# A choice of experts without GpSimd arithmetic, a gather ahead of the first weight splits, and buffers cleared on ScalarE

## The chip, the cores and the metric

The kernel runs on one core of a Trainium2 chip. The metric is device time in microseconds, from the first to the last instruction and what lies around them; shorter is better. The engines are called as the profile calls them: PE (TensorE, matmuls), DVE (VectorE), ACT (ScalarE), POOL (GpSimd) and SP (SyncE). Each has a queue of instructions of its own and works through it in order. DMAs are issued from the queues of SP, ACT and POOL. What an engine needs from another it waits for on semaphores.

## The reference

One step of an encoder layer over 576 tokens: 512 frames of one stream and 64 of another. The first half mixes tokens (sparse attention and a convolution branch). The second half is a mixture of experts, and the change lies where the one passes into the other:

```python
x = layer_norm(ALPHA * x + (1 + g1) * mix, ln1_g, ln1_b)
h2 = x * (1 + sc2) + sh2
# hier_moe(h2): the best of 4 groups, in it the best 2 of 4 experts
gl = hf @ w_group + b_group;  g_idx = argmax(gl);  g_w = max(softmax(gl))
rl = hf @ w_router + b_router
top_val, top_idx = lax.top_k(in_group, 2)
w_top = softmax(top_val) * g_w
# per expert: silu(h @ gate) * (h @ up) * weight, then @ down, summed over the two
x = layer_norm(ALPHA * x + (1 + g2) * moe, ln2_g, ln2_b)
```

There are 16 experts; each has a gate-and-up matrix of 1024 x 512 and a down matrix of 256 x 1024. All is float32.

## The kernel before

Tokens lie in five tiles of 128 (the last has 64), `t` = 0 to 4. Products that need full precision split each float32 operand into a rounded high part and a low part: `split_into` copies the high part on ACT (L139) and subtracts it on DVE (L140), and `mm3` (L144 to L146) makes three matmuls of them.

*Around the choice.* For each tile, `ln1` normalises the rows `xn[t]` and multiplies them with the routers on PE (L849); L850 adds the bias on DVE. `h2_rows` (L856) scales the rows on DVE and sums them with a DMA of POOL into the scratch tensor `h2_scr` (L857), from which the experts gather. `ax_rows` multiplies `xn[t]` by ALPHA's row in place (L900) and sums it with a DMA of POOL into `z_scr` (L901), the start of the final residual. Tiles 0 and 1 multiply on DVE, tiles 2 to 4 on POOL. `route` then picks groups, experts and places with many small DVE operations (L919 to L978), once for tiles 0 to 2 and once for tiles 3 and 4. Its result for the four fixed experts is `idt` (L1011, called `routed` in the code). The exponential for the weights is on ACT (L1030), and L1031 on DVE waits for it. Further DVE operations (L1054 to L1074) put the other twelve experts in order of their size; `order` (L1072) is read by SP, which then loads the weights of the experts it names.

*Experts.* `gather` (L1125) fetches up to 128 rows of `h2_scr` into one of three buffers `xg`; POOL makes its descriptors. The buffers are cleared first (L1080, on POOL). Two of them lie in the buffers of `h2`, so they wait for the DMAs of `h2_rows`. `table` then writes the slot of every token with ten small scatters from POOL (L1263). `rows_in` transposes the gathered rows on PE (L1140), copies the high part on ACT (L1145) and subtracts on DVE (L1146), all into `xhl`. An expert's gate-and-up product goes in four quarters (`step`, six matmuls each); `hidden` (L1163, L1164), `turned` (L1170), `down` (L1188) and a scatter-add into `z_scr` (L1203) follow. On PE the next expert's first two quarters come ahead of the turn and the down product of the one before.

*Weights.* Six 512 KB pieces per expert stream through a ring of 24 places (six buffers of four). A gate-and-up piece is split ahead by `split_ahead`: three sets of split buffers are free at the start (`room[False]`), and a fourth, which lies in the buffers of `xn[4]` and `ohr`, counts as `room[True]`. The fourth split therefore waits for the DMA that sums `xn[4]` into `z_scr`. When a piece has been split, SP loads a later expert's piece into its place.

*Slots.* One pool of seven large buffers holds the ring's six and `xhl`. The last ring buffer takes the place of `rows1`, which L856 reads last. `xhl` takes that of `xn03`, which holds `xn[0]` to `xn[3]`; in the compiled program its first write, L1145, waits for the four DMAs of L901 that sum these tiles.

*Order.* A planner orders each engine's queue by program order and by when its own cost model has an instruction ready. `issue_after(ins)` queues a block's instructions behind `ins` on that engine and is no wait. `manual_schedule` keeps the expert part of PE, DVE and ACT in the order written. In the compiled program POOL's queue runs: sums of `h2` and `z` with the three multiplications and the clears among them, the three first gathers, the ten scatters of the table.

Of the kernel before, what the change touches and what calls it, by code (L numbers as in the profile page):

```python
# [10 lines left out]
F32 = mybir.dt.float32  # L11
# [3 lines left out]
AF = mybir.ActivationFunctionType  # L15
OP = mybir.AluOpType
# [8 lines left out]
NT = 5  # L25
# [33 lines left out]
def encoder_step(ctx: ExitStack, tc: tile.TileContext, a, o):  # L59
    nc = tc.nc  # L60
    V, S, G, PE, SY = nc.vector, nc.scalar, nc.gpsimd, nc.tensor, nc.sync
# [67 lines left out]
        raw_load[0] = (eng or SY).dma_start(raw, src).ins  # L129
        return raw  # L130

    raw_load, split_copy = [None], [None]

    def split(raw, shape, tag="w", bufs=3):
        return split_into([wp.tile(shape, F32R, name=tag + p, tag=tag + p, bufs=bufs) for p in ("hi", "lo")], raw)
# [1 line left out]
    def split_into(parts, raw):  # L137
        hi, lo = parts
        split_copy[0] = S.copy(hi, raw).ins  # L139
        V.tensor_tensor(lo, raw, hi, op=OP.subtract)  # L140
        return hi, lo

    def mm3(out, lh, ll, rh, rl, start, stop):
# [750 lines left out]
    ax_sums = []  # L894


    def ax_rows(t, behind):
        n = TS[t]
        with tc.issue_after(behind):
            (G if t > 1 else V).tensor_tensor(xn[t][0:n], xn[t][0:n], axr[0:n], op=OP.mult)  # L900
            ax_sums.append(G.dma_start(dap(z_d, t * 128 * D, [[D, n], [1, D]]), xn[t][0:n], accum_op=OP.add).ins)  # L901

    mb = late.tile([128, NT + 1, 16], BF, name="mb", bufs=1)
# [76 lines left out]
    for t in range(NT):  # L980
        n = TS[t]
        sl = slice(128 * t, 128 * t + n)
        po = acc("o1")
        if t == 4:
            with tc.issue_after(trs[1]):
                for k0 in range(0, KT, 2):
                    sample_product(po, k0, 2, ms, *wo[k0 // 2])
        else:
            for k in range(KT):
                wh, wl = wo[k // 2]  # L990
                mm3(po, mh[:, k, sl], ml[:, k, sl], wh[:, k % 2, :], wl[:, k % 2, :], k == 0, k == KT - 1)
        residual(t, po, 1)
        ln1(t)
        if 0 < t < 4:
            h2_rows(t - 1)
            if t < 3:
                ax_rows(t - 1, normed[-1][0])
    ohr = late.tile([128, 2, NT, 128], F32R, name="ohr", tag="ohr", bufs=1)
    route(0, 3)
    h2_rows(3)  # L1000
# [15 lines left out]
    routed = token_columns(pid[:, 0:NFIX], 0, NFIX)  # L1016
    pids = late.tile([128, 2, NVAR], F32, name="pids", tag="bw", bufs=1)
    V.tensor_copy(pids[:, 0, :], pid[:, NFIX:NE])

    for t in range(2, NT):  # L1020
        ax_rows(t, routed)


    w12 = late.tile([128, NT, 2], F32, name="w12", bufs=1)
# [52 lines left out]

    xg = [late.tile([128, D], F32, name="xg", tag=tag, bufs=2) for tag in ("h2", "h2", "xg")]
    for x in xg:
        G.memset(x, 0.0)  # L1080


    ring = []
# [174 lines left out]
    def table():  # L1258
        V.tensor_copy(pay.bitcast(F32)[:, :, :, 1], w12)
        for t, j in [(t, j) for t in range(NT) for j in range(2)]:  # L1260
            n = TS[t]
            with tc.issue_after(gathers[2]), tc.issue_after(ax_sums[-1]):
                st = G.indirect_dma_start(out=ids_d, out_offset=bass.IndirectOffsetOnAxis(ap=slt[0:n, t, j:j + 1], axis=0),  # L1263
                                          in_=pay[0:n, t, j, :], in_offset=None)
            for other in scat:
                tc.declare_no_dep(st.ins, other.ins, reason="every slot is given to one row")
            scat.append(st)
# [68 lines left out]
                load_down(number(n), k, n.down[k])  # L1336

    steps = [(x, c) for x in units for c in range(4) if len(x.experts) == 1]
    room = {False: 3, True: 1}
    owed = [0]  # L1340


    def split_ahead():
        while steps and len(steps[0][0].experts[0].gate_up) > steps[0][1]:
            x, c = steps[0]
            fourth = room[False] <= owed[0]
            if not room[fourth]:
                return
            steps.pop(0)
            room[fourth] -= 1  # L1350
            x.parts.append([next_split(x.experts[0].gate_up[c], fourth)])
            x.sets.append(fourth)
            follow_gate_up(x.experts[0], c)

    def gather_next():
        n = len(gathers)
        for x in units:
            for b, ar in x.blocks:
                if b == n:
                    return gather(b, ar[0])  # L1360
# [12 lines left out]
        x.parts, x.sets = [], []  # L1373
    LA = 2
    load_first(2)
    for _ in range(3):
        gather_next()
    table()
    with tc.manual_schedule(engines={mybir.EngineType.PE, mybir.EngineType.DVE, mybir.EngineType.Activation}):
        first_loads(3)  # L1380
        with tc.issue_after(routed):
            split_ahead()
        rows_in(0)
        pend, over = [], overflow()

        def product(p):
            p.y = gate_row(p.ar[2], p.ar[3])
            p.pd = down(p.hT, p.dns)
            for y in p.experts:
                y.left -= 1  # L1390
                if y.left == 0:
                    follow_down(y)
            add_rows(p.y, p.pd, p.ar[0])

        for u, x in enumerate(units):
            if u == 2:
                for y in units:
                    i = y.es[0] - NFIX
                    if 0 <= i < NPAIR:
                        c = G.value_load(order[0:1, NVAR + i:NVAR + i + 1], min_val=3 * (NE + NFIX), max_val=3 * (2 * NE - 1))  # L1400
                        y.blocks[1] = (y.blocks[1][0], place_ids(c, G))
                    if len(y.es) == 2:
                        y.blocks[0] = (y.blocks[0][0], static_args(y.es))
                token_columns(cols[:, 0, NFULL:NVAR], NFIX + NFULL, NE)
            owed[0] = int(u + 1 < len(units) and len(units[u + 1].es) == 2)
            blocks = []
            for b, _ in x.blocks:
                p = Unit()
                p.b, p.experts = b, x.experts
                p.ar = dict(x.blocks)[b]  # L1410
                p.dns = [y.down for y in x.experts]
                blocks.append(p)
            for y in x.experts:
                y.left = len(blocks)
            nxt = units[u + 1].blocks[0][0] if u + 1 < len(units) else None

            def step(c, p, last=True):
                if c == 0:
                    p.pg = acc("pg")
                if len(x.experts) == 1:  # L1420
                    gate_up(p.pg, p.b, c, x.parts[c])
                else:
                    gate_up(p.pg, p.b, c, [y.gate_up[c] for y in x.experts])
                    for y in x.experts:
                        follow_gate_up(y, c)
                if c == 3:
                    p.hm = hidden(p.pg, p.ar[1])
                if u > NFIX and not (u + c) % 2:
                    next(over, None)
                if last:  # L1430
                    freed(c)

            def freed(c):
                if len(x.experts) == 1:
                    room[x.sets[c]] += 1
                elif c == 3:
                    room[False] += 1
                split_ahead()

            def rows(b):  # L1440
                if b is not None:
                    whole = any(len(y.es) == 2 and y.blocks[0][0] == b for y in units)
                    if whole:
                        assert room[False]
                        room[False] -= 1
                        owed[0] = 0
                    rows_in(b, whole)
                    if len(gathers) <= b + LA:
                        gather_next()

            def turn_next(i):
                if i < len(pend):
                    pend[i].hT = turned(pend[i].hm)

            def product_next(i):
                if i < len(pend):
                    product(pend[i])

            if len(blocks) == 1:
                p = blocks[0]  # L1460
                step(0, p)
                step(1, p, False)
                turn_next(0)
                freed(1)
                rows(nxt)
                product_next(0)
                turn_next(1)
                step(2, p)
                product_next(1)
                step(3, p)  # L1470
            else:
                p, q = blocks
                step(0, p, False)
                rows(q.b)
                step(1, p, False)
                turn_next(0)
                turn_next(1)
                product_next(0)
                step(0, q)
                step(1, q)  # L1480
                product_next(1)
                step(2, p, False)
                step(3, p, False)
                rows(nxt)
                step(2, q)
                step(3, q)
            pend = blocks
        rows3 = slot([128, 2, D], name="rows3")
        brow(rows3[:, 0], a["ln2_g"], 0, SY)
        brow(rows3[:, 1], a["ln2_b"], 0, SY)  # L1490
        for i in range(len(pend)):
            turn_next(i)
            product_next(i)
# [83 lines left out]
```

## Time and profile before

| | us |
|---|---|
| median of 3 runs (860.08 to 865.51) | 863.53 |
| the profiled execution's own time | 862.35 |
| its span, first to last instruction | 860.7 |
| PE busy | 774.9 (90%) |
| DVE busy | 639.8 (74%) |
| ACT busy | 358.3 (42%) |
| POOL busy | 137.9 (16%) |

The profile is one execution. A row of a timeline gives the start, the length in us, the engine, the line, the operation with its output and inputs, how many were merged, and in brackets how long the engine stood idle before it and what ended that. A row of the chain of waits gives the start, the length, and what the program's end waited for at that time. Groups of instructions give the count, the busy time and the mean in ns of one. Waits are put down to what came last by the profile's own inference.

### The profile page before, as it was taken

The page shows a single profiled execution, that of the slowest core. Times are in us where ns is not written, and L with a number is a line of the kernel's source. Part 1 is how long each engine was busy: PE and PEld are TensorE (multiplying, and loading weights), DVE is VectorE, ACT ScalarE, POOL GpSimd, SP SyncE. Part 2 cuts the span into 40 slices and gives each one's busy share as a digit, 9 for nine tenths or more (in the row PEclk, how much of TensorE's full clock was granted, in tenths as well). Part 3 has the DMA queues.
Part 4 walks back from the last instruction along what each step waited for, and adds up shares of the span by engine and source line. Part 5 has one row for each costly group of instructions (what it writes and reads, how often), then busy time and mean ns, then how long its engine had stood idle before and what let it go on. Part 6 is the DMA issues. An engine that isn't in the chain of part 4 may idle for free.

```text
span 860.7 us, 13259 instructions
## 1 busy us (share of the span) xinstructions
PE 774.9 (90%) x4827; PEld 633.9 (74%) x4827; DVE 639.8 (74%) x1255; ACT 358.3 (42%) x654; POOL 137.9 (16%) x172
## 2 busy tenths in 40 slices
PE   4899999999999999999999999999835999999910
PEld 3788888887878989988999799978734676645400
DVE  1569999989998999999995426539793886555416
ACT  3243232333335435568633943312423664434205
POOL 2300000300200000000100001110556223212220
PEclk9999999999999999999999999999857899999965
DMA  9997754482432333343433108585996998799425
GB/s 290 340 365 236 223 175 150 114 226 82 144 107 74 101 91 103 91 127 92 130 103 103 40 1 299 200 268 162 222 307 164 342 360 275 206 353 378 130 49 200
DMA packets 108865, 159.70 MB, mean 186 GB/s; under 512 B 9714, under 2 KB 67210, under 8 KB 108800
## 3 DMA queue, kind: packets, MB, share of 16 engines
q1 hardware_dynamic: 94464, 120.38, 42.9%
q0 software_dynamic: 12736, 34.26, 15.4%
q10 hardware_dynamic: 1600, 4.22, 1.3%
q8 instruction: 38, 0.62, 0.3%
q14 instruction: 27, 0.22, 0.1%
HBM read 143.65 MB, written 26.13 MB: 197 GB/s over the span
## 4 chain that ended last, share of the span: by engine, by line
PE 56%; DVE 10%; DMA 4%; ACT 3%; issue 2%; another core or an unknown queue 1%; POOL 0%; POOLq 0%; SPq 0%; DVEq 0%; ACTq 0%
PE acc L242 6%; PE acc L244 6%; PE acc L243 6%; PE pd L1188 5%; PE pg L144 3%; PE pg L146 3%; PE pg L1158 3%; PE pg L145 2%; PE tm L144 2%; PE po L673 2%; PE tm L146 2%; PE tm L145 2%; DMA z_scr<-yo,idt 2%; PE pxt L1140 2%; PE o L144 2%
## 5 line engine op out<-in xcount | busy, mean ns | idle before, releaser
L600 DVE SCALAR_TENSOR_TENSOR y<-ue,dwT,y 128x604 f32<-128x604 f32 (+17 forms) x232 | 183.4, 827 | 1.9 <-ACT y L598 1.5
L242 PE MATMUL acc<-hh,wlo 128*128 128x288 f32 (+1 forms) x504 | 152.7, 303 | 1.4 <-DVE wlo L140 1.4
L243 PE MATMUL acc<-hh,whi 128*128 128x288 f32 (+1 forms) x504 | 149.9, 298 | 0.0
L244 PE MATMUL acc<-hl,whi 128*128 128x288 f32 (+1 forms) x504 | 148.5, 298 | 0.0
L139 ACT CAST whi<-wraw 128x1024 fp32r<-128x1024 f32 (+1 forms) x72 | 75.1, 1045 | 159.6 <-PE acc L244 72.9
L140 DVE TENSOR_TENSOR wlo<-wraw,whi 128x1024 fp32r<-128x1024 f32 (+1 forms) x72 | 87.4, 1214 | 38.1 <-ACT whi L139 38.0
L242 PEld LDWEIGHTS acc<-hh,wlo 128*128 128x128 f32 (+1 forms) x504 | 94.3, 187 | 16.7 <-issue 8.7
L243 PEld LDWEIGHTS acc<-hh,whi 128*128 128x128 f32 (+1 forms) x504 | 94.3, 187 | 2.8 <-issue 2.6
L244 PEld LDWEIGHTS acc<-hl,whi 128*128 128x128 f32 (+1 forms) x504 | 93.6, 187 | 2.3 <-issue 2.1
L140 DVE TENSOR_TENSOR wlo<-ring,whi 128x1024 fp32r<-128x1024 f32 x30 | 36.4, 1223 | 21.3 <-ACT whi L139 20.8
L144 PE MATMUL tm<-wlo,hh 128*128 128x512 f32 x128 | 50.5, 397 | 0.4 <-DVE wlo L140 0.4
L145 PE MATMUL tm<-whi,hh 128*128 128x512 f32 x128 | 50.4, 394 | 0.0
L146 PE MATMUL tm<-whi,hl 128*128 128x512 f32 x128 | 49.8, 392 | 0.0
L139 ACT CAST whi<-ring 128x1024 fp32r<-128x1024 f32 x30 | 31.3, 1049 | 34.3 <-PE pg L146 23.3
L1188 PE MATMUL pd<-ring,hT 128*128 128x512 f32 x96 | 44.4, 606 | 1.0 <-ACT hT L1172 0.5
L242 PE MATMUL acc<-oh,wlo 128*128 128x288 f32 x128 | 38.6, 302 | 1.5 <-DVE gt L757 1.1
L242 PE MATMUL acc<-yh,wlo 128*128 128x288 f32 x128 | 38.4, 301 | 0.1
L243 PE MATMUL acc<-yh,whi 128*128 128x288 f32 x128 | 38.4, 301 | 0.0
L244 PE MATMUL acc<-yl,whi 128*128 128x288 f32 x128 | 38.2, 302 | 0.1
L1203 POOL DMA_INDIRECT z_scr<-yo,idt x16 | 26.5, 1656 | 73.2 <-DMA z_scr<-yo,idt 29.7
L243 PE MATMUL acc<-oh,whi 128*128 128x288 f32 x128 | 38.0, 298 | 0.0
L244 PE MATMUL acc<-ol,whi 128*128 128x288 f32 x128 | 37.8, 298 | 0.0
(474 smaller groups left out, 1743.7 us busy)
## 6 DMA issues: line engine op xcount, KB each, us to landing
ring<-in_w_gate_up_dram SPq DMA_DIRECT2D x62, 512.0 KB
wraw<-in_w_in_dram SPq DMA_DIRECT2D x48, 512.0 KB
wada<-in_w_ada_dram SPq DMA_DIRECT2D x32, 512.0 KB
ring<-in_w_down_dram SPq DMA_DIRECT2D x32, 512.0 KB
wada<-in_w_ada_dram SPq DMA_DIRECT2D x32, 256.0 KB
gates_scr<-glg POOLq DMA_DIRECT2D x16, 288.0 KB
gt<-gates_scr POOLq DMA_DIRECT2D x16, 288.0 KB
wraw<-in_w_conv_out_dram SPq DMA_DIRECT2D x8, 512.0 KB
```

The costliest lines, as they stand in the source:

```text
L139: split_copy[0] = S.copy(hi, raw).ins
L140: V.tensor_tensor(lo, raw, hi, op=OP.subtract)
L144: PE.matmul(out, lh, rl, start=start, stop=False)
L145: PE.matmul(out, lh, rh, start=False, stop=False)
L146: PE.matmul(out, ll, rh, start=False, stop=stop)
L242: PE.matmul(ps[h][0:m, 0:288], wl[:, k, :], xh[:, k, sl], start=k == 0, stop=False)
L243: PE.matmul(ps[h][0:m, 0:288], wh[:, k, :], xh[:, k, sl], start=False, stop=False)
L244: return PE.matmul(ps[h][0:m, 0:288], wh[:, k, :], xl[:, k, sl], start=False, stop=k == KT - 1).ins
L600: V.scalar_tensor_tensor(y[:, 30 - i:EXT], ue[:, 0:EXT - 30 + i], dwT[:, j, i:i + 1], y[:, 30 - i:EXT], op0=OP.mult, op1=OP.add)
L1158: PE.matmul(p[half], xwhole[b][:, k, half], ws[i][:, 512 * (k % 2):512 * (k % 2) + 512], start=k == 0, stop=k == KT - 1, tile_position=(0, ...
L1188: PE.matmul(pd_[c], hT[:, k, :], dns[0][k][:, cs], start=k == 0, stop=k == 1)
L1203: sc = G.indirect_dma_start(out=z_d, out_offset=bass.IndirectOffsetOnAxis(ap=idx[0:128 // len(ids)], axis=0), in_=y[half], in_offset=None, ...
```

## The change

- `ax_rows` multiplies on DVE for all tiles. Tile 2's call moves into the loop over tiles, behind the normalisation of tile 3. Those of tiles 3 and 4 move behind the first three gathers in the program, and their multiplications wait for a marker.
- The marker is a memset of one element on POOL, queued behind the first gather.
- The subtractions of the splits made before the first expert starts wait for the marker too. Once those are issued, the list of what to wait for is emptied.
- The three `xg` buffers are cleared on ACT, by a copy with scale 0 of a constant.
- The fourth set of split buffers is not to be had at the start; it is from the second expert (`u == 1`) on.

```diff
-    raw_load, split_copy = [None], [None]
+    raw_load, split_copy, split_behind = [None], [None], []
+
+    def wait_for(ins, others):
+        for other in others:
+            tc.add_manual_dep(ins, other.name,
+                              mybir.DependencyInfo(mybir.DependencyClass.Sync, mybir.DependencyReason.DATA),
+                              reason="the first gather's descriptors are made first")
...
-        V.tensor_tensor(lo, raw, hi, op=OP.subtract)
+        wait_for(V.tensor_tensor(lo, raw, hi, op=OP.subtract).ins, split_behind)
...
-    def ax_rows(t, behind):
+    def ax_rows(t, behind, others=()):
         n = TS[t]
         with tc.issue_after(behind):
-            (G if t > 1 else V).tensor_tensor(xn[t][0:n], xn[t][0:n], axr[0:n], op=OP.mult)
+            wait_for(V.tensor_tensor(xn[t][0:n], xn[t][0:n], axr[0:n], op=OP.mult).ins, others)
...
             h2_rows(t - 1)
-            if t < 3:
-                ax_rows(t - 1, normed[-1][0])
+            ax_rows(t - 1, normed[-1][0])
...
-    for t in range(2, NT):
-        ax_rows(t, routed)
...
     for x in xg:
-        G.memset(x, 0.0)
+        S.activation(x.rearrange("p (r n) -> p r n", r=8), iota128[:, None, :].to_broadcast([128, 8, 128]), AF.Copy, scale=0.0)
...
-    room = {False: 3, True: 1}
+    room = {False: 3, True: 0}
...
-    for _ in range(3):
+    gather_next()
+    made = late.tile([1, 1], F32, name="made", bufs=1)
+    with tc.issue_after(gathers[0]):
+        split_behind.append(G.memset(made, 0.0).ins)
+    for _ in range(2):
         gather_next()
+    for t in range(3, NT):
+        ax_rows(t, routed, split_behind)
     table()
...
             split_ahead()
+        split_behind.clear()
...
         for u, x in enumerate(units):
+            room[True] += u == 1
```

## The prediction

> **What bounds the kernel now.** I read the page for the span, then a table of stretches, the chain of waits, and the timelines of GpSimd (POOL), VectorE (DVE), ScalarE (ACT) and SyncE around the choice of experts.
>
> ```profile
> span 860.7 us, 13259 instructions
> ...
> 605.00:647.00 42.00, 24.11 (x157) 21.55 (x156) 35.57 (x131) 12.94 (x19) 23.08 (x16) 0.65 0.98 269
> 647.00:667.00 20.00, 12.27 (x52) 9.66 (x50) 7.24 (x14) 6.58 (x8) 13.08 (x14) 0.76 0.69 169
> 667.00:800.00 133.00, 131.03 (x553) 80.14 (x554) 90.90 (x127) 66.62 (x96) 31.94 (x24) 0.98 0.95 320
> ```
>
> The columns are length, then busy time of PE, PE's loads, DVE, ACT and POOL, granted clock, DMA share and GB/s. From 667 to 800 PE works 131 of 133 us: the experts are bound by PE, and whatever reaches PE earlier there ends earlier. The change can only shorten 605 to 667: first the choice (DVE busy 35.6 of 42 us), then the first two experts, where PE stands still 7.7 of 20 us. The chain of waits through both stretches:
>
> ```profile
> 613.73 1.83 DVE xn L810
> 619.90 2.76 DVE t L921
> ...
> 628.59 2.31 DVE sj L973 x2
> 630.90 0.83 DVE rki L974
> ...
> 635.10 0.43 DVE w L1031
> ...
> 639.01 7.48 DMA xg<-h_scr,idt
> ...
> 654.21 0.23 PE pg L146
> ...
> 659.24 5.15 another core or an unknown queue
> ```
>
> Small DVE operations with long times lie on the chain. GpSimd's and DVE's own timelines show why:
>
> ```profile
> 598.24 0.92 POOL L857 DMA_DIRECT2D h_scr<-h  x1 [35.75 <-DVE h L856]
> ...
> 619.95 2.66 POOL L900 TENSOR_TENSOR xn<-xn,axr 128x1024 f32<-128x1024 f32 x1
> ...
> 627.56 0.85 POOL L857 DMA_DIRECT2D h_scr<-h  x1 [3.79 <-DVE rk L961]
> ...
> 634.56 0.94 POOL L1080 MEMSET xg<- 128x1024 f32 x1 [2.02 <-DMA h_scr<-h]
> 639.01 4.45 POOL L1125 DMA_INDIRECT xg<-h_scr,idt  x1 [3.51 <-DVE M L1057]
> 643.77 1.76 POOL L1125 DMA_INDIRECT xg<-h_scr,idt  x1 [0.31 <-issue]
> 645.83 1.00 POOL L1125 DMA_INDIRECT xg<-h_scr,idt  x1 [0.30 <-issue]
> 647.13 1.03 POOL L1263 DMA_INDIRECT ids_scr<-pay,slt  x1 [0.30 <-issue]
> ```
>
> ```profile
> 602.26 1.22 DVE L900 TENSOR_TENSOR xn<-xn,axr 128x1024 f32<-128x1024 f32 x1
> ...
> 613.01 0.69 DVE L809 TENSOR_TENSOR rt<-o,rows 128x512 f32<-128x512 f32 x1 [1.20 <-PE o L160]
> ...
> 624.47 0.16 DVE L850 TENSOR_TENSOR rlog<-prt,brs 64x20 f32<-64x20 f32 x1
> ...
> 631.85 0.16 DVE L921 TENSOR_TENSOR t<-ing,m 128x8 f32<-128x8 f32 x1
> ...
> 636.51 0.22 DVE L973 SCALAR_TENSOR_TENSOR sj<-sj,rk 128x2 f32<-128x2 f32 x2
> 636.65 0.16 DVE L974 CAST rki<-rk 128x4 int32<-128x4 f32 x1
> ...
> 638.99 3.47 DVE L140 TENSOR_TENSOR wlo<-ring,whi 128x1024 fp32r<-128x1024 f32 x3
> ...
> 643.39 1.22 DVE L140 TENSOR_TENSOR gs<-ring,gs 128x1024 fp32r<-128x1024 f32 x1
> ...
> 649.93 0.17 DVE L1072 TENSOR_SCALAR order<-rank 128x12 int32<-128x12 f32 x1
> ```
>
> L921 takes 2.76 us until GpSimd's multiplication ends at 622.61, and 0.16 when GpSimd is quiet. The reverse holds at 639: the first gather takes 4.45 us, and it ends 1.00 us after the three subtractions, a gather's own time.
>
> **The choice, part by part.** The stalls on the chain, each less its undisturbed twin (L809 for L810, L974's 0.16 for L1031): 1.83-0.69, 2.76-0.16, 2.31-0.22, 0.83-0.16, 0.43-0.16: 1.14+2.60+2.09+0.67+0.27 = 6.8 us. GpSimd's arithmetic and clears cause them, and both go.
>
> ```profile
> L900 POOL TENSOR_TENSOR xn<-xn,axr 128x1024 f32<-128x1024 f32 (+1 forms) x3 | 7.7, 2558 | 1.6 <-issue 1.6
> L901 POOL DMA_DIRECT2D z_scr<-xn x5 | 4.4, 872 | 0.8 <-POOL xn L900 0.6 <-DVE xn L900 0.3
> ...
> L1178 ACT ACTIVATE yo<-gr,sel 128x1024 f32<-128x1024 f32 x13 | 15.1, 1163 | 0.0
> ...
> 620.46 1.89 PE L849 MATMUL prt<-wrs,h2T 128*64 128x20 f32 x16
> ```
>
> What comes in: the third multiplication moves to DVE (1.22). DVE is idle 1.20 us ahead of L809, but the tile is ready only late in that gap: I charge 0.7, between 0 and 1.22. With L810 then 0.4 us earlier and L921 2.6 shorter, DVE reaches L850 at 621.4; PE's logits, 0.4 earlier too, end at 621.9: 0.5 lost. The clears cost ACT three times some 1.2 us (L1178 as the nearest row); ACT is busy 12.9 of 42 us, so they lie beside other work, unless one stands in ACT's queue ahead of the exponential that L1031 waits for: 0 to 1.2, I take 0.3. Net 6.8-0.7-0.5-0.3 = 5.3: the gather starts at 633.7. It also needs the last h2 rows in memory. They land at 634.5 now; their L857 goes 2.5 us earlier, so 632.0, which still hides.
>
> **The gate on the subtractions.** The gather then takes 1.00 instead of 4.45 and ends at 634.7 instead of 643.46: 8.8 us gained so far. Behind the marker's memset (0.3 with its gap) five DVE operations with two SBUF inputs wait: three subtractions (3.47) and the multiplications of tiles 3 and 4 (2x1.22). All else on DVE is queued behind them. They run to 640.9, and now the second gather meets them: it was held through three in a row at 639, so I let all five hold it.
>
> A rule of the Trainium skill speaks against the gate (SBUF — State Buffer, Who interferes with whom): a tensor_tensor takes only the read interface shared with GpSimd, while making descriptors needs the write interface, so it should not stall a DMA. The same list says that an operation with two SBUF inputs contends with GpSimd's reads, and a gather reads its indices from SBUF. The trace sides with the second: 1.76 us for the gather at 643.77, with the subtraction of 643.39 running, 1.00 for the next. By the first the gate buys nothing.
>
> **What takes the stall's place.** The first experts' input, xhl, lies in the slot of the pool that xn03 leaves, so its first write (L1145) waits for the z sums of tiles 0 to 3. Today they are long in memory. After the change tile 3's sum is issued on GpSimd behind three gathers: second gather 640.9+1.0, third 0.3+1.0, then 0.3+0.87: 644.4.
>
> ```profile
> 602.00:603.00 1.00, 1.00 (x6) 0.80 (x5) 1.00 (x2) 1.00 (x3) 0.36 (x1) 1.00 0.74 143
> 603.00:604.00 1.00, 1.00 (x7) 0.84 (x5) 0.47 (x1) 0.89 (x1) 0.74 (x2) 1.00 0.00 0
> ```
>
> The same kind of sum, issued at 598.24 into empty queues, was still moving 143 GB/s before 603 and nothing after: 3.8 us from the end of its record. So tile 3 lands at 648.2. Bounds: if the second gather is not held, 642.3; if the queues are as full as for the sum of 627.56 (634.5-628.4 = 6.1), 650.5. I take 648.2, as the loads of j=3 are in by then.
>
> ```profile
> 647.69 0.58 ACT L1145 CAST xhl<-pxt 128x512 fp32r<-128x512 f32 x1 [7.84 <-DMA xg<-h_scr,idt]
> ...
> 658.65 0.58 ACT L1145 CAST xhl<-pxt 128x512 fp32r<-128x512 f32 x1 [4.17 <-PE pg L146]
> 664.74 1.04 ACT L139 CAST whi<-ring 128x1024 fp32r<-128x1024 f32 x1 [5.50 <-remote]
> ```
>
> L1145 starts at 647.69 now, so 0.5 us later: all of the 8.8 is gone again.
>
> **The first two experts.** ACT stands still 4.17 and 5.50 us around 658 with no releaser that fits, and SyncE creeps at the same time:
>
> ```profile
> L1096 SPq FUSED_REGOPS  x1: 702/702/702, 653.6 to 653.6; - x1
> ...
> L1096 SPq FUSED_REGOPS  x48: 13/46/702, 651.5 to 785.2; - x48
> ```
>
> A register step of 46 ns takes 702. What causes this hold I cannot read off. If it follows the ten scatters of the slot table (647.13), it comes 1.2 us earlier, since they start at 645.9 behind the z sums; if it follows SyncE's waking by `order` (649.93), which then stands some 2.5 us behind the five operations, 6.5 us. I take 5, nearer to the second, as SyncE is slow soon after waking. Against it: only three splits are in hand, not four, so the fourth and its successor must be cast and subtracted when PE already wants them: two times 1.22, 2.5 lost (0 if the hold has passed by then). In sum +0.5-5+2.5 = -2.0 us. The profiled execution (862.35, of which 1.65 lies outside the span) becomes 860.4, the median of the runs, 863.53, becomes 861.5. Everything later moves with it, bound by PE.
>
> **Rivals.** (1) The sum of tile 3 does not gate: GpSimd slips in between the DVE operations, at the bound 642.3. The gather itself (634.7, 3.0 to land by 7.48-4.45, at most 6.1, then 1.15 to L1145) allows 641.9. 5.4 gained instead of 0.5 lost: 855.6. For it speaks that reductions with one input may fall among the five; against it 3.47 without a gap. (2) The hold goes away or falls into the wait for the z sum: some 7 of PE's 7.7 idle us, 863.5+0.5-7 = 857, with (1) 851. Nothing in the profile says that it must recur. (3) Slower: the hold stays where it is, from 654.5. It decides from the point where PE's first step ends too late for the fourth split to be cast ahead of it, as with L1145 at 650.5. PE then stops after 18 matmuls (three quarters of an expert, six each) instead of 36; 18 times 0.23 is 4.2, and the two late splits 2.5: 870. (4) DVE is not what held the gather: it still ends 3.45 later, 638.2, but the gathers behind it aren't held by the five either (1.76 and 1.0): the sum is out at 642.7 and lands at 646.5, 1.2 early. 863.5-1.2-2.5 = 859.8. That is what the skill's first rule would make of it.
>
> **How the numbers follow.** Forecast 0.45, own range 856 to 866; rivals 0.20, 0.15, 0.15, 0.05. About 1% (8.6 us) is what a measurement here can tell from no change. Faster than 854.9 needs most of (1) with an earlier hold, or (1) and (2) together: 0.20. Slower than 872.2 needs (3) and a further delay: 0.10. The rest, 0.70, is within 1%. The range 852 to 868 leaves out the joint case of (1) and (2) and most of (3).
>
> **What would show it.** Right: L921 and L973 at 0.2 us; no L900 or L1080 on POOL; the first gather near 634 with 1.0 us; the second one long; L1145's first wait ended by the z sum, not by the gather; PE's first expert at about 648 as before. Wrong: L1145 released by the gather (then 1), no idle ACT between the first two experts (2), PE idle ahead of the fourth split (3), a long first gather in spite of the gate (4).

## The result, and the profile after

The changed kernel takes 853.82 us (median of 4 executions, 853.15 to 857.59), the kernel before, beside it, 864.52. The ratio is 0.9895, with a 95% interval of 0.9848 to 0.9941. A second comparison (12 executions of the changed kernel, 35 of the one before) gave 0.9943, 0.9904 to 0.9981. So the change gains between half a per cent and one, about what a measurement of this kernel can tell. The prediction was 861.5 in a range of 852 to 868. The time lies in that range, but outside the 856 to 866 that the forecast itself had been given, and the gain came in other places than forecast. The profiled execution of the changed kernel took 853.15 (862.35 before).

The page and the table of stretches of the changed kernel, in the columns of the prediction:

```profile
span 851.5 us, 13261 instructions
...
605.00:647.00 42.00, 25.68 (x163) 22.74 (x161) 31.36 (x135) 14.63 (x21) 13.34 (x13) 0.67 0.99 273
647.00:667.00 20.00, 15.12 (x58) 11.42 (x59) 11.37 (x17) 11.76 (x16) 15.35 (x15) 0.76 0.68 188
667.00:800.00 133.00, 132.07 (x558) 78.94 (x558) 91.45 (x128) 64.51 (x91) 32.61 (x22) 1.00 0.95 325
```

VectorE works 4.2 us less in the choice. PE works 15.1 of 20 us in the first two experts instead of 12.3, and ScalarE 11.8 instead of 6.6: the holes there are mostly closed. VectorE's timeline in the choice (start, length, engine, line, operation; in brackets the idle time before it and what ended it):

```profile
619.68 0.17 DVE L927 TENSOR_TENSOR t<-ing,m 128x12 f32<-128x12 f32 x1
...
626.06 0.22 DVE L979 SCALAR_TENSOR_TENSOR sj<-sj,rk 128x3 f32<-128x3 f32 x2
...
633.10 0.17 DVE L1033 TENSOR_SCALAR w<-w 128x5 f32<-128x5 f32 x1 [3.08 <-ACT w L1032]
...
638.03 2.35 DVE L906 TENSOR_TENSOR xn<-xn,axr 128x1024 f32<-128x1024 f32 x2 [0.63 <-issue]
640.31 3.48 DVE L146 TENSOR_TENSOR wlo<-ring,whi 128x1024 fp32r<-128x1024 f32 x3
```

The two long operations (2.76 and 2.31 us) are short. But VectorE now stands 3.08 us for the exponential. ScalarE's timeline shows what is ahead of it:

```profile
624.42 3.29 ACTq L1098 DMA_DIRECT2D ring<-in_w_gate_up_dram  x2
629.08 1.06 ACT L1082 ACTIVATE xg<-iota 128x1024 f32<-128x1024 f32 x1 [5.72 <-DVE sj L978]
630.04 2.92 ACT L145 CAST whi<-ring 128x1024 fp32r<-128x1024 f32 x3
632.87 0.20 ACT L1032 ACTIVATE w<-w 128x5 f32<-128x5 f32 x1
...
650.16 1.07 ACT L1147 CAST xhl<-pxt 128x512 fp32r<-128x512 f32 x2 [16.14 <-DMA z_scr<-xn]
653.81 1.04 ACT L145 CAST whi<-ring 128x1024 fp32r<-128x1024 f32 x1 [2.58 <-issue]
656.37 1.05 ACT L145 CAST whi<-ring 128x1024 fp32r<-128x1024 f32 x1 [1.51 <-PE pg L152]
```

The issue of two ring loads keeps ScalarE until 627.71 (3.29 us; before it took 1.26, from 627.30 on). The clear of the first xg then waits until 629.08 for the rows of h2 to land: its buffer was h2's, and though the row names VectorE, the semaphore of that DMA steps last at 629.00. Behind it come three split casts, and only then the exponential. In the second profile of this kernel (below) the rows had landed before the loads were issued (633.17 against 633.88), and still the exponential came 28.2 us after the first z sum, against 28.7 here. So the wait for the landing is the smaller part of it. Further down, the first copy into xhl is ended by the z sum, as predicted, and the two holes around 658 are gone. GpSimd's and PE's timelines:

```profile
636.81 1.11 POOL L1127 DMA_INDIRECT xg<-h_scr,idt  x1 [11.27 <-DVE M L1059]
637.91 0.09 POOL L1381 MEMSET made<- 1x1 f32 x1
638.22 1.97 POOL L1127 DMA_INDIRECT xg<-h_scr,idt  x1 [0.22 <-issue]
640.50 1.91 POOL L1127 DMA_INDIRECT xg<-h_scr,idt  x1 [0.31 <-issue]
642.41 1.96 POOL L907 DMA_DIRECT2D z_scr<-xn  x2
644.66 1.14 POOL L1265 DMA_INDIRECT ids_scr<-pay,slt  x1 [0.30 <-issue]
```

```profile
650.80 0.80 PE L150 MATMUL pg<-wlo,xhl 128*128 128x512 f32 x1 [7.63 <-ACT xhl L1147]
...
663.32 0.38 PE L1172 MATMUL pht<-ident,hm 128*128 128x128 f32 x2
```

The first gather ends at 637.92 instead of 643.46. Yet PE's first expert matmul comes at 650.80 instead of 648.33, so up to here the change has lost 2.5 us. The first turn (pht) comes 12.5 us after that matmul, where it took 19.7 (648.33 to 668.05). PE's last down product ends at 817.4 instead of 823.1, another 1.0 gained (behind the hold PE's granted clock was 0.50 from 662 to 672, and the first down product took 4.53 us; now the clock is 1.00 there and the product takes 3.70), and from there to the end of the span it is 34.1 us instead of 37.6. In sum +2.5-7.2-1.0-3.5 = -9.2, the difference of the spans. The last of these terms shows in the chain of waits, which before ran through PE until 810. In the changed kernel, asked from 605 to 815, it starts only at 775 and holds nothing but scatter-adds into z_scr, each waiting for the one before:

```profile
775.56 1.42 DMA z_scr<-yo,idt
...
782.81 9.33 DMA z_scr<-yo,idt
```

**How the runs are compared.** Executions of one kernel differ by 10 us and more, and the profiles show where: at the same VectorE instruction six of them (the first profiles of the two kernels, and the runs on the gate, the clears, the buffers and the missing table) agree within 1.0 us up to 522, and lie up to 7.2 apart at 593, in a stretch that no kernel here changes. So each profile is read from its own first z sum (the first `z_scr<-xn` on GpSimd). The table gives, in us from there, the start of the first gather, the first xhl copy and PE's first expert matmul; then the time from that matmul to the first pht, from there to the end of PE's last down product, from there to the end of the span, and the sum of the last four. The last column is the ratio to the kernel before, measured beside it, with its interval.

| kernel | first z sum at | gather | xhl | PE | to pht | to last down | to end | sum | ratio |
|---|---|---|---|---|---|---|---|---|---|
| before | 603.8 | 35.2 | 43.9 | 44.5 | 19.7 | 155.1 | 37.6 | 256.9 | |
| before, again | 603.2 | 35.2 | 44.0 | 44.7 | 19.4 | 154.9 | 36.4 | 255.4 | 1.002 (0.997 to 1.006) |
| changed | 604.1 | 32.7 | 46.1 | 46.7 | 12.5 | 154.1 | 34.1 | 247.4 | 0.990 (0.985 to 0.994) |
| changed, again | 609.5 | 32.2 | 46.0 | 46.6 | 13.1 | 154.1 | 34.6 | 248.5 | 0.994 (0.990 to 0.998) |
| no gate | 609.2 | 32.2 | 49.6 | 50.2 | 12.2 | 154.1 | 33.9 | 250.4 | 0.997 (0.993 to 1.001) |
| clears behind | 609.3 | 32.4 | 46.8 | 47.5 | 12.5 | 154.0 | 36.9 | 250.9 | 1.000 (0.996 to 1.004) |
| fourth set | 607.6 | 32.0 | 50.1 | 50.8 | 12.3 | 153.1 | 33.6 | 249.8 | 0.996 (0.993 to 1.000) |
| buffers exchanged | 603.9 | 30.3 | 35.9 | 36.5 | 10.6 | 163.3 | 33.7 | 244.1 | 0.993 (0.990 to 0.997) |
| table behind | 604.4 | 30.2 | 35.8 | 36.4 | 10.6 | 159.5 | 42.7 | 249.2 | 0.997 (0.993 to 1.001) |
| scatter first | 607.5 | 31.4 | 37.1 | 37.7 | 12.4 | 154.1 | 34.3 | 238.5 | 0.983 (0.979 to 0.987) |
| before, no table | 611.0 | 34.7 | 43.5 | 44.1 | 10.9 | 153.5 | 33.8 | 242.3 | 0.989 (0.980 to 0.997) |
| before, loads wait | 607.0 | 35.1 | 44.1 | 44.8 | 19.5 | 155.1 | 41.3 | 260.6 | 1.002 (0.998 to 1.005) |
| before, sums behind | 604.3 | 35.0 | 54.5 | 55.2 | 11.8 | 153.4 | 33.7 | 254.0 | 1.005 (1.002 to 1.007) |
| before, scatter first | 608.7 | 35.2 | 44.0 | 44.6 | 19.7 | 154.8 | 33.6 | 252.7 | 0.993 (0.991 to 0.996) |

Read this way the change gains 8.2 us (mean of the two sums before, 256.2, less that of the two after, 248.0).

### The profile page after: what moved, and what is told of

It is laid out like the page before. It is cut to its first block, busy times and chain, and to the rows that moved or that the text cites. A ratio compares the mean times of both kernels' runs of the same rounds, so it can differ in the third digit from the quotient of the medians.

```text
span 851.5 us, 13261 instructions
## 1 busy us (share of the span) xinstructions
PE 777.2 (91%) x4827; PEld 635.5 (75%) x4827; DVE 636.0 (75%) x1258; ACT 361.4 (42%) x657; POOL 128.4 (15%) x167
## 5 line engine op out<-in xcount | busy, mean ns | idle before, releaser
L146 DVE TENSOR_TENSOR wlo<-ring,whi 128x1024 fp32r<-128x1024 f32 x32 | 38.9, 1223 | 14.7 <-ACT whi L145 12.6
L145 ACT CAST whi<-ring 128x1024 fp32r<-128x1024 f32 x32 | 33.2, 1046 | 23.2 <-PE pg L152 19.9
L150 PE MATMUL pg<-wlo,xhl 128*128 128x512 f32 x76 | 33.7, 444 | 7.9 <-ACT xhl L1147 7.6
```

What stands on the lines that cost most here:

```text
L146: wait_for(V.tensor_tensor(lo, raw, hi, op=OP.subtract).ins, split_behind)
L150: PE.matmul(out, lh, rl, start=start, stop=False)
```

## The experiments

**Do both profiles repeat?** Each kernel ran once more, unchanged.

> The kernel before, once more, with a profile of its own. The first z sum's issue on GpSimd is the common clock (603.83 in the first profile, 256.9 us ahead of the end). Theory A (the hold in the first two experts belongs to this order of work): from PE's first expert matmul to the first turn (pht) 19 to 20 us again, undisturbed 10.6 to 12.5 as in the other kernels; first z sum to the end 255 to 258 us. Theory B (the hold comes in some executions only): 11 to 13 us, and 248 to 250 us to the end.

> The changed kernel, once more. Theory A (its order keeps the hold away): PE's first expert matmul to pht 12 to 13 us as in its first profile, first z sum to the end 246 to 251 us. Theory B (the hold was absent by chance): 19 to 20 us, 254 to 258 us to the end. In both, the first xhl copy comes 46 us after the first z sum, released by the z sum of tile 3.

ScalarE's timeline in the second profile of the kernel before has the hold at the same place, to 0.2 us when counted from the first z sum:

```profile
657.91 0.59 ACT L1145 CAST xhl<-pxt 128x512 fp32r<-128x512 f32 x1 [4.16 <-PE pg L146]
663.97 1.04 ACT L139 CAST whi<-ring 128x1024 fp32r<-128x1024 f32 x1 [5.47 <-remote]
```

To pht it took 19.4 us, in the changed kernel 13.1. Theory A both times: the hold belongs to an order of work, not to chance. The trace's semaphore records say what ScalarE waits for there: PE's counter steps at 653.64 in the first profile of before, then not until 658.63 and 664.38, though PE's matmuls run without a gap from 653.50 to 659.27. ScalarE's copy starts 20 ns behind the step of 658.63, and its next wait ends 30 ns behind that of 664.38. What is late is not the work but its signal (some records may be missing, so this is a reading, not a count).

**Does the gate pay?** The marker is written, and nothing waits for it.

```diff
-        split_behind.append(G.memset(made, 0.0).ins)
+        G.memset(made, 0.0)
```

> The changed kernel without the gate: the marker is written, and nothing waits for it, so the multiplications of tiles 3 and 4 and the three subtractions may run while the first gather's descriptors are made. Theory A (the z sum sets the start of the experts, gate or no gate): the first gather takes 3 to 4.5 us instead of 1.1, the two behind it 1.0, the z sums are issued by 643 to 645, first xhl copy at 649 to 651, 853 to 855 us, the same. Theory B (the gate buys what the gather's length shows): 3 us later throughout, 856 to 858 us.

GpSimd's timeline:

```profile
641.43 4.44 POOL L1127 DMA_INDIRECT xg<-h_scr,idt  x1 [10.57 <-DVE M L1059]
```

The gather takes 4.44 us again, and the first xhl copy comes 3.6 us later than with the gate (49.6 against 46.0). That is Theory B. I had thought the z sum would land at a time of its own; it is issued behind the gathers, and so whatever holds a gather holds the sum too. (The semaphore of tile 3's sum steps last at 658.61, and the copy starts at 658.77; the profile's own inference names a scatter of the table there.) So the gate is worth 3.6 us at the experts' start and 2 to 3 at the end by the sums; the intervals of the ratios overlap. By the Trainium skill's rule that the prediction weighed (SBUF — State Buffer, Who interferes with whom) a subtraction could not hold the making of descriptors, which the page itself marks as inferred. The gather's 4.44 us, against 1.11 with the five operations out of the way, speak against it.

**What does the clear ahead of the exponential cost?** All three clears go behind the exponential.

```diff
     for x in xg:
-        S.activation(x.rearrange("p (r n) -> p r n", r=8), ...)
+        with tc.issue_after(weighed):
+            S.activation(x.rearrange("p (r n) -> p r n", r=8), ...)
```

> The changed kernel with the three clears queued on ACT behind the exponential. Theory A (the clear ahead of the exponential waits for the h2 sums and costs what the prediction had put at 0.3): exponential at about 630.5 instead of 632.9, first gather at 634.5 instead of 636.8, the z sums and PE's start 2.3 us earlier, 851.5 us. Theory B (the landing of the z sums follows the queues and not the time of issue): gather earlier, xhl at 650 as before, 853 to 854 us.

```profile
636.55 0.17 DVE L1033 TENSOR_SCALAR w<-w 128x5 f32<-128x5 f32 x1 [1.89 <-ACT w L1032]
```

Theory B as to the time, but for another reason. The exponential comes 1.2 to 1.7 us earlier against the first z sum, yet VectorE still waits 1.89 for it, since the three casts are still ahead. And the planner, which orders VectorE's queue by its own costs, now put L1033 ahead of the small operations that had filled this time, so the gather starts no earlier (32.4). Its tail is longer besides (36.9 against 34.1 and 34.6): the planner laid the scatter-adds as in the kernel before, of which more below. The clear was only one of three things in that queue. Where the next run but one moved ScalarE's two ring loads and the casts as well, the exponential came at 24.7 instead of 28.7 and the gather 2 us earlier.

**Are three splits in hand dearer than four?**

```diff
-    room = {False: 3, True: 0}
+    room = {False: 3, True: 1}
...
-            room[True] += u == 1
```

> The changed kernel with the fourth set of split buffers to be had from the start, as before the change. Theory A (the prediction's term: three splits in hand instead of four cost 2.5 us): PE's first expert matmul to pht falls from 12.5 to about 10 us; the fourth cast waits for the z sum of tile 4 and stands ahead of the first xhl copy, which comes 1.0 to 1.5 us later; in sum 1 to 1.5 us faster. Theory B (three are enough): 12 to 12.5 us as before, and 1 to 1.5 us slower in all.

```profile
656.79 1.04 ACT L145 CAST gs<-ring 128x1024 fp32r<-128x1024 f32 x1 [19.95 <-DMA z_scr<-xn]
```

Theory B: 12.3 us to pht with four sets, 12.5 and 13.1 with three. The fourth cast waits for the last z sum and stands ahead of the xhl copy, which comes 4.1 us later (1.0 to 1.5 expected).

**Does the z sum alone hold the experts' start?** xhl and the last ring buffer change places: a slot is given at first use, so the loads into that ring buffer go behind the first `rows_in`, and all of them to SP.

```diff
-            if j == 3 and c >= 2:
-                load_gate_up(j, c, piece(j, c), S)
-            else:
-                load_gate_up(j, c, piece(j, c))
+            if c == 2:
+                yield
+            load_gate_up(j, c, piece(j, c))
...
-        first_loads(3)
+        rest = first_loads(3)
+        next(rest)
...
         rows_in(0)
+        next(rest)
...
-    for x in xg:
+    for i, x in enumerate(xg):
+      with tc.issue_after(weighed if i else turned_rows[0]):
```

> The changed kernel, with xhl and the last ring buffer in each other's places: the loads of j=3 that use the last ring buffer come behind the first rows_in, all on SP, so xhl takes the buffer of rows1 and only the ring waits for the sums of tiles 0 to 3; the clears of the second and third xg are queued behind the exponential. Theory A (the z sum alone held the first xhl, and what follows moves with it): exponential at 630.1 instead of 632.9, first gather at 634.1, landed 3.0 after its end, first xhl copy at 639 to 640 instead of 650.2, PE's first expert 10 to 11 us earlier, 843 us. Theory B (another bound lies right behind: the hold of PE's signals around the ten scatters of the table, or the chain of the scatter-adds into z_scr, which ends the changed kernel): first xhl copy as early as in A, but less than half of it is left at the end, 849 to 854 us.

The first copy comes 35.9 us after the first z sum instead of 46.1, ended by the transposes of the gathered rows: the z sum was the gate. Some 2 of the 10 come from the earlier gather, 8 from the exchange. But at the end only some 4 us are left, Theory B. The hold is not back (10.6 to pht). The loss lies between 662 and 681, in PE's and VectorE's timelines:

```profile
667.79 1.94 PE L1143 MATMUL pxt<-ident,xg 128*128 128x128 f32 x8 [5.32 <-DMA xg<-h_scr,idt]
```

```profile
672.23 0.15 DVE L1276 CAST so<-ido 128x1 f32<-128x1 int32 x1 [10.13 <-DMA ido<-ids_scr]
```

The fourth expert's gather stands on GpSimd behind the table's ten scatters and starts only at 658.93, and VectorE, in order, stands 10 us for rows read from that table, which it needs an expert or two later. PE's granted clock is 0.50 from 666 to 672, where it had been 1.00 before the gap. PE has run into what used to be early enough.

**The table behind the fourth gather.** The run before, with the scatters of the table moved behind that gather and its reading one expert later.

```diff
-            with tc.issue_after(gathers[2]), tc.issue_after(ax_sums[-1]):
+            with tc.issue_after(gathers[3]), tc.issue_after(ax_sums[-1]):
...
-    table()
+    V.tensor_copy(pay.bitcast(F32)[:, :, :, 1], w12)
...
                 rows(nxt)
+                if u == 0:
+                    table()
...
-            if u == 2:
+            if u == 3:
                 for y in units
```

> The changed kernel with xhl and the last ring buffer in each other's places and the clears of the second and third xg behind the exponential, as in the run on the buffers, and besides with the ten scatters of the slot table behind the fourth gather on GpSimd, and the reading of that table one expert later. Theory A (in the run on the buffers the 9 us lost between 662 and 681 come from the table standing ahead of the fourth gather on GpSimd, and from VectorE waiting in order for the table's rows): first pht 47 us after the first z sum as there, the next three 10 to 11 us apart, PE's last down product 701 us or less, 735 us or less from the first z sum to the end counted from the program's start at the same first z sum, 838 to 842 us in all. Theory B (the serial chain of the scatter-adds or the loads of the ring bound the end): first experts as in A, but the end only 0 to 4 us ahead of the run on the buffers, 844 to 848 us at the same first z sum.

The first experts go as hoped (pht at 651.4, 662.5, 672.6, 683.2), and yet the sum is 249.2, worse than the run before it: Theory B's chain, and by more than it had allowed (853 us at the same first z sum, where 844 to 848 were expected). GpSimd's timeline has the cause:

```profile
711.08 1.31 POOL L1128 DMA_INDIRECT xg<-h_scr,idt  x1 [4.37 <-PE pxt L1143]
712.70 1.60 POOL L1206 DMA_INDIRECT z_scr<-yo,idt  x1 [0.30 <-DVE hits L1243]
```

The planner placed three gathers, the last of them waiting for PE's transposes, ahead of the fourth scatter-add. The scatter-adds wait for one another, some 10 us each here, so a late one makes all later ones late, and the stretch after PE's last product grows to 42.7. The same pair of rows stands in the first two kernels, one way round before,

```profile
728.16 1.31 POOL L1125 DMA_INDIRECT xg<-h_scr,idt  x1 [4.34 <-PE pxt L1140]
729.77 1.61 POOL L1203 DMA_INDIRECT z_scr<-yo,idt  x1 [0.30 <-DVE hits L1240]
```

and the other way round after:

```profile
718.43 1.59 POOL L1205 DMA_INDIRECT z_scr<-yo,idt  x1 [0.31 <-DVE xhl L1148]
722.45 1.35 POOL L1127 DMA_INDIRECT xg<-h_scr,idt  x1 [2.44 <-PE pxt L1142]
```

**The place of the scatter-adds.** Each later gather is queued behind the last scatter-add before it in the program, once on the run above and once on the kernel before, alone.

```diff
+        if ordered and scatters:
+            with tc.issue_after(scatters[-1]):
+                ga = fetch()
```

> The kernel of the run with the table behind the fourth gather, with each later gather on GpSimd queued behind the last scatter-add into z_scr that comes before it in the program. Theory A (there the planner had put gathers, which wait for PE's transposes, ahead of the fourth and fifth scatter-add, and the chain of scatter-adds, each waiting for the one before, then ended 8 us later against PE): first pht 47 us after the first z sum, PE's last down product 154 us after that instead of 159.5, from there to the end 34 us instead of 42.7; 235 us from the first z sum to the end instead of 249.2, 839 to 842 us at the same first z sum. Theory B (the chain is bound by the landing of each scatter-add and not by its place in the queue): 159 and 42 us again, 849 us from the first z sum on, as there.

> The kernel before with that one edit alone: each later gather queued behind the last scatter-add before it in the program. Theory A (3 us of the change's gain are the place of one scatter-add ahead of one gather, which the planner chose anew and the change did not ask for): hold in the first experts as before (19 to 20 us from PE's first expert matmul to pht), PE's last down product to the end 34 us instead of 36.4 to 37.6, 252 to 254 us from the first z sum to the end instead of 255.4 to 256.9. Theory B (the end goes by PE): 36 to 38 us again.

Theory A in both. On the kernel before, the tail is 33.6 us instead of 36.4 to 37.6, with the hold untouched (19.7), and the ratio is 0.9934 (0.9907 to 0.9960). So some 3 us of the change's gain are a choice of the planner that the change did not ask for, and by the ratios this edit alone brings about as much as the whole change did in its second comparison; by the sums it is 3.5 us against 8.2. The run with the clears behind, with the order of the kernel before and its longer tail, fits this. So the end of the kernel before hung on the scatter-adds as well, although its chain of waits runs through PE until 810. That chain passes from PE to the scatter-adds at this row:

```profile
813.96 1.57 POOL L1203 DMA_INDIRECT z_scr<-yo,idt  x1 [2.86 <-DVE yo L1199]
```

The wait is put down to VectorE, but it is as long as those of the next but one and the last scatter-add (2.83 and 2.74 us), which the profile puts down to the landing of the one before.

On the combined kernel PE's last product comes 154.1 us after pht and the end 34.3 after that; the sum is 238.5 instead of 249.2 (235 expected; the first pht comes 50.1 us after the first z sum and not 47). At 849.77 us (ratio 0.983, 0.979 to 0.987) it beats both kernels: 18 us less than before by the sums, 1.7% by the medians.

**What causes the hold?** First, the kernel before without the table's scatters.

```diff
-        for t, j in [(t, j) for t in range(NT) for j in range(2)]:
+        for t, j in []:
```

> The kernel before without the ten scatters of the slot table (the table keeps its first contents, so the rows beyond an expert's first places are left out of the result; gathers and scatters of those blocks move no rows). Theory A (these scatters cause the hold of 650 to 665): ACT's idle 4.17 and 5.50 us go, the first turn (pht) comes at about 661 instead of 668.05, SP's register steps stay at 50 ns, 856 to 858 us. Theory B (the hold follows SP's waking by order and its first loads with a register address): all stays where it was, 861 to 865 us.

SyncE's register steps (FUSED_REGOPS, arithmetic for the address of a load; count, then shortest, median and longest in ns) and ScalarE's timeline:

```profile
L1096 SPq FUSED_REGOPS  x48: 43/46/56, 657.9 to 781.5; - x48
```

```profile
660.84 1.07 ACT L1145 CAST xhl<-pxt 128x512 fp32r<-128x512 f32 x2
662.44 1.05 ACT L139 CAST whi<-ring 128x1024 fp32r<-128x1024 f32 x1 [0.53 <-ACT xhl L1145]
```

Theory A: no step above 56 ns, no hole, 10.9 us to pht. Without the scatters there is no hold. Next, whether SyncE's loads have to run among them.

```diff
+            if not held:
+                tc.add_manual_dep(ld, scat[-1].ins.name, ...)
+                held.append(ld)
```

> The kernel before with one wait more: SyncE's first load with a register address waits until the last of the table's ten scatters has landed. Theory A (the hold needs SyncE's loads with a register address among those scatters): from PE's first expert matmul to pht 11 to 13 us instead of 19.4 to 19.7; with the ring filled some 13 us later a later expert may wait. Theory B (the scatters alone hold the signals up, whatever SyncE does): 19 to 20 us again.

```profile
661.79 0.59 ACT L1145 CAST xhl<-pxt 128x512 fp32r<-128x512 f32 x1 [3.74 <-PE pg L146]
...
667.87 1.04 ACT L139 CAST whi<-ring 128x1024 fp32r<-128x1024 f32 x1 [5.49 <-remote]
```

Theory A fell: with no load of SyncE in the whole stretch (it only reads `order` into registers, which no run took out) the holes are 3.74 and 5.49 us, and SyncE's own steps still take 0.7 us each until 667.5. That is 60.5 us after the first z sum, as in the first profile of before (664.4). The sum is 4 us longer, all of it in the tail (41.3), which was not followed up. Last, one step of the change alone on the kernel before: the sums of tiles 3 and 4 between the gathers and the table.

```diff
-        ax_rows(t, routed)
+        ax_rows(t, routed, t < 3)
...
         gather_next()
+    for t in range(3, NT):
+        with tc.issue_after(gathers[2]):
+            ax_sums.append(G.dma_start(dap(z_d, ...), xn[t][0:TS[t]], accum_op=OP.add).ins)
     table()
```

> The kernel before with one step of the change alone: the DMAs that sum tiles 3 and 4 into z_scr are issued behind the first three gathers, straight ahead of the table's ten scatters; multiplications and clears stay on GpSimd, no gate, four sets of split buffers. All kernels so far with the sums ahead of the gathers show the hold (19.4 to 19.7 us from PE's first expert matmul to pht), all with the sums between gathers and table do not (10.6 to 13.1). Theory A (that place of the sums, with their transfers running while the scatters start, is what takes the hold away): first xhl copy 51 to 53 us after the first z sum instead of 44, pht 11 to 13 us after PE's first expert matmul; in sum about as long as before. Theory B (another part of the change takes it away): xhl as late as in A and the hold of 19 to 20 us besides, so 7 us slower.

ScalarE's and PE's timelines, and SyncE's reads of `order` (count, then shortest, median and longest in ns):

```profile
657.87 1.04 ACT L139 CAST gs<-ring 128x1024 fp32r<-128x1024 f32 x1 [23.68 <-DMA ids_scr<-pay,slt]
```

```profile
671.17 0.38 PE L1171 MATMUL pht<-ident,hm 128*128 128x128 f32 x2
```

```profile
L1322 SPq TENSOR_LOAD <-order x8: 261/264/273, 660.6 to 664.6; - x8
```

Theory A: 11.8 us to pht. The price is a later first xhl copy, 54.5 instead of 43.9, and so the whole is no faster (1.005). As in the run with the fourth set, the fourth cast stands ahead of that copy; the profile names a scatter of the table for its wait, but the semaphore of tile 4's sum steps last at 657.85. The experts now start late among the scatters, so SyncE is the better witness: 12 to 16 us after the first scatter its reads of `order` take 0.26 to 0.27 us each (the last row above), where the kernel before had steps of 0.7 us until 17 us after it. Of 14 profiles, the four with the sums ahead of the gathers and the table in place show the hold, the nine with the sums straight ahead of the table (or one gather away) do not, whether the experts start before the table, as in the three runs with exchanged buffers, or at its end, as here. Why scattered writes hold up other engines' signals when they run by themselves, and not when 0.75 MB of sums run beside their start, no run here settles. The table's packets are 64 bytes in the trace. The Trainium skill (DMA: Bandwidth & Descriptors, Specifications) says that below 512 bytes a DMA reads, modifies and writes; no run shows that this is the cause. Spacing the scatters out, or making their rows larger, was not tried.

## Why the prediction was right or wrong

- **The stalls, 6.8 us less 0.7 and 0.5.** Right. L927 and L979 take 0.17 and 0.22 us, the wait for the logits is 0.46. VectorE is through with all that lies ahead of the exponential at 630.0 instead of 635.0: 5.0 gained, 5.6 predicted.
- **The clear ahead of the exponential, 0.3, at most 1.2.** Wrong, and out of its bounds: VectorE waits 3.08. I priced the clear by its length and not by what stands in its queue. There two ring loads are ahead of it, it can wait for a landing, and three casts of 2.92 us in all follow it, and only then the exponential. The run with the clears behind gives 1.2 to 1.7 for the clear itself; the rest is the loads and the casts, which stood ahead of the exponential before as well (628.60 to 631.54) but were done when VectorE, then slower, came to need it. The row that would have shown the landing is the clear's own wait before, 2.02 us for `h_scr` on GpSimd, which I had quoted.
- **The gather, 1.00 us behind the gate.** Right: 1.11, and 4.44 without the gate.
- **Five operations hold the second gather to 640.9.** Wrong in the mechanism: it takes 1.97 us and the third 1.91, each about one operation longer than alone. GpSimd gets in between VectorE's operations. This more than made up for the late start of the first gather (636.81, not 633.7): the record of tile 3's sum, 1.02 us long from 642.41 on, ends at 643.4, where 644.4 was predicted. That this came out so near is luck, by two errors that cancel.
- **The z sum gates xhl, at 648.2 (642.3 to 650.5).** Right in the mechanism, which was the heart of the forecast: the copy is released by `z_scr<-xn` at 650.16, and with another buffer it comes 10 us earlier. I took 3.8 us to land, by the sum that had met empty queues, and 6.1 as the other bound; it took 6.6 (the semaphore of tile 3's sum steps last at 650.01). So 650.16 lies within 642.3 to 650.5 only because the sum was out 1.0 us early.
- **The hold, 5 earlier, and 2.5 lost to fewer splits.** Wrong. It did not come earlier, it went: 19.7 to 12.5 us, 7.2 gained, which is the second rival's mechanism (0.15). And three splits cost nothing. The prediction called the hold's cause unreadable and shifted it with `order`; the runs show that it needs the table's scatters and not SyncE's loads, and that the sums of tiles 3 and 4 straight ahead of the table take it away (19.4 to 19.7 us without, 11.8 with them). This term was mis-sized by 4.7 us net, the largest error.
- **Everything later moves with it, bound by PE.** Wrong by 4.5 us: 1.0 up to PE's last product, with the clock, and 3.5 behind it (2.7 in the mean of two profiles each). From 775 on the end goes by the chain of scatter-adds, which I did not weigh, and its place in GpSimd's queue changed with the edit.
- **The sum.** Predicted +0.5-5+2.5 = -2.0 us, measured +2.5-7.2+0-1.0-3.5 = -9.2. The time fell into the range of 852 to 868 because rivals were counted into it, chiefly the second (857, to which the scatter-adds' part came), and not because the forecast's own path came true. For that path it was luck.

So the forecast (little or no gain, the choice's gain given back at the z sum) describes what happens up to 651 us, and the 8 us of gain come from two things that the change was not made for: the hold and the place of one scatter-add.

## What to carry to other kernels

Price a moved operation by the queue it joins: what it waits for there, and what stands behind it until it is done. When a gate or a wait is taken away, look at buffers that change hands: here some 8 us of the experts' start hung on which of two tiles inherits a buffer from a slow DMA. Where a planner orders a queue, compare the order of every queue after an edit, also far from it; one exchange of a scatter-add and a gather was worth some 3 of the 8 us.

## What the runs showed of the hardware

- Ten small scatters from GpSimd, with nothing beside them, held up PE's signals to ScalarE by 4 to 6 us and stretched most steps of SyncE in that time to some 700 ns (a register step takes 46), in four profiles out of four. With the table left out this was gone, and with two sums (0.75 MB together) issued just before it the holes did not come, while a few of SyncE's steps stayed slow (a register step of up to 687 and 696 ns in the two profiles of the changed kernel).
- How a gather comes through a row of two-input VectorE operations is not settled. The second and third gather of the changed kernel took 1.97 and 1.91 us beside five in a row, each about one operation longer than alone; the first gather of the kernel before, beside three in a row, took 4.45, three operations longer, and that of the changed kernel without the gate 4.44.
- A matmul of the first expert takes 0.63 us at first and 0.39 later. In the changed kernel that lasts until 656, 5 us, in the run with exchanged buffers until 642.2, 2 us, in the combined kernel until 650.9, 6 us, with nearly the same order of work. It is the granted clock: 0.50 in the stretches 654 to 656, 638 to 640 and 648 to 650 of these three profiles, and 1.00 from 658, 642 and 652 on. That is about the difference between 10.6 and 12.5 us to pht. What sets the moment of the step, no run here was made to show.
